# An MLP's first products for eight of sixteen groups placed in front, and the loads behind it put in another order

## The chip, the cores and the metric

The kernel runs on one core of a Trainium2 chip. The metric is the device time of one execution in microseconds. A core has TensorE (PE in the profile: matmuls and transposes, with PEld for its weight loads), VectorE (DVE), ScalarE (ACT), GpSimd (POOL) and SyncE (SP, which here only issues DMAs), each with its own queue of instructions that it works off in order, and 16 DMA engines.

## The reference

Two blocks run one after the other on 1024 tokens of width 1024: a hybrid layer with four attention-like branches, and a block that mixes, then applies an MLP and a gated projection. Only the end of the second block is touched:

```python
h = h + rms_norm_2(mix, g_mix_post[i])
hn = rms_norm_2(h, g_mlp_pre[i])
ff = jnp.square(jax.nn.relu(hn @ w_up[i])) @ w_down[i]      # 1024 -> 4096 -> 1024
h = h + rms_norm_2(ff, g_mlp_post[i])
gate = jax.nn.sigmoid(rms_norm_2(h, g_ple_pre[i]) @ w_ple_gate[i])
e = (p[i] @ w_ple_proj[i]) * gate
h = h + rms_norm_2(e, g_ple_post[i])
```

## The kernel before

**Products.** Every product is made in three matmuls: each operand is split into a high part (a rounded copy, `copy` at L147) and a low part (what is left, `sub_lo` at L157 on DVE or L155 on POOL), and high x high, high x low and low x high are summed in PSUM. Both big products of the MLP use a scheme with seven block products in place of eight; operands are formed as sums and differences of blocks on DVE.

**Order of the work.** The program is written in order, and a planner then lists the instructions of each engine: what stands earlier in the text has the higher priority, but an instruction whose inputs or buffer are not there by the planner's own clock is passed by. So loads written later can be issued earlier where a buffer is free. `issue_after` ties instructions of one engine behind a given one. All DMAs of the MLP are issued on SP's queue, except a few on ACT's.

**Buffers.** Tag "blk" has 31 slots of 4 KB a partition (`blk`, L93), shared by activations, operands, raw weights and norm tiles. Tag "w" has 9 slots (`NW`). PSUM banks come from four tags: "mm" 2, "s" 2, "t" 3, "o" 1. Pools opened for a stage take over the memory of the stage before once its tiles have been read.

**Before the MLP.** `out_phase` ends the mixing; `to_T` (L1201) transposes the first four token tiles into `hn`, eight slots of "blk". `t_pair` (L1655) reads two token tiles back, forms the operands t1 to t4 and b22 as differences (L1667 to L1670), transposes them (L274) and splits them: five operands of four slots each.

**Lead** (L1708 to L1720). For the first `LEAD` = 4 of 16 groups of 128 columns the two products that need only `hn` (`up_p1`, `up_p2`) are made ahead, while `t_pair` works; the results stay in `pa` (4 buffers).

**Up** (`up_group`, L1733). Each group loads its two weight halves (`wu`, 2 buffers, L1737), forms four sums (L1740 to L1743), makes the remaining products (five where the lead made two, else seven), evacuates them, applies relu and square, forms four combinations on POOL (L1786 to L1789), and stores seven arrays of 256 KB (L1792). The groups run from 0 to 15.

**Down** (L1881 to L1929). Two stages (groups 0 to 7, then 8 to 15) of seven products, with 96 matmuls each (L1919 to L1921). A stage loads sixteen 512 KB tiles of `w_down` (L1889), then for each product and quarter a left tile (L1908), and splits both. `evac_down` adds the products into `acc` (L1837). The products of a stage stand in the order

```python
order = (("a11", "b11"), ("s2", "t2"), ("s3", "t3"), ("a22", "t4"), ("s1", "t1"), ("s4", "b22"), ("a12", "b21"))
```

**Norm and gate.** After the fifth product of stage two the token tiles 4 to 7 are complete: `finish_mlp` (L1815) reads the residual, multiplies by the gain on POOL (L1824), scales and adds on DVE (L1827), and norms for the gate (L1225); its transposes follow the next product. Tiles 0 to 3 come after the last product. `ple_weights` (L1803) loads and splits a half of the gate's weights: half 0 ahead of the sixth product in "blk" slots (raw, high and low: twelve), half 1 at the end in "w" slots. Then sixteen gate products (24 matmuls each) run by tile, 4 to 7 and 0 to 3, with `evac_ple` (L1937) and `finish_ple` (L1950).

Of the kernel before, what the change touches and what calls it, by code (L numbers as in the profile page):

```python
# [27 lines left out]
_T = dict(STA='s', XN1=0, PWT=1, PO='0x1', PO2={}, PS=2, PSX=0, PSE='a', PB=99, PEA=(0, 1, 4), WB=8, XL=3, CLO='p', STE=None, STW=None, ST1='b', ST2='b', PLP='pvv', WLO2='p', QXP=1, LW='vp', LEAD=4, FD={0: 'g', 1: 'b', 6: 'g'}, FW=(0, 2), AG=0, PREO=(0, 2, 1), PMB=0, PWB=1, PM=3, SG=2, FA={(0, 2): 'g', (0, 3): 'mmm', (0, 7): 'qm', (1, 0): 'gg', (1, 6): 'gz'}, FB={(0, 3): 'm', (0, 7): 'qm', (1, 3): 'm', (1, 5): 'z', (1, 7): 'm'}, FC={(0, 3): 'mm', (0, 7): 'q', (1, 3): 'zm', (1, 6): 'm'}, NORM='v', NORM2='v', CS=8, MM=2, SB=2, TB=3, OB=1, WHI='aaav', WLO='pv', PTH='a', NW=9, NBLK=31, PTB=2, XN=1, AS=(2, 4, 6, 7), CPP=2, CALT=1, WORK='s0 A A A A A A A A s1 q t B c B B c c B p w B 5 6b c c c 4 0a 1a g 6a 7 3a 2 e e c c c B e B c B 1b e 0b 3b', KS=(2, 0, 3, 1))  # L28
# [48 lines left out]
def hybrid_then_mix_kernel(ctx: ExitStack, tc, I, c1, c2, out, dbg=None, upto=99):  # L77
# [1577 lines left out]
    def t_pair(t):  # L1655
# [15 lines left out]
        for name, src in (("t1", d[:, k1]), ("b22", xb[:, k2]), ("t2", e[:, k1]), ("t3", d[:, k2]), ("t4", e[:, k2])):  # L1671
# [6 lines left out]
            for kp in range(2):  # L1678
                s3 = tp[:, kp * 256:kp * 256 + 256].rearrange("p (k t) -> p k t", k=2)
                copy(hi[kp][:, :, o:o + P], s3, "a")  # L1680
                sub_lo(lo[kp][:, :, o:o + P], s3, hi[kp][:, :, o:o + P], "v")

# [25 lines left out]
    lead = []  # L1708
    for g in range(_T["LEAD"]):
# [23 lines left out]
    def up_group(g):  # L1733
# [10 lines left out]
        if g >= len(lead):  # L1744
# [4 lines left out]
            pa, a = up_tile(), mmb()  # L1749
            up_p1(pa, a, wa)  # L1750
        else:
            pa = lead[g]
        h23, s23 = wslot((2, 4, P)), wslot((2, 4, P))
        copy(h23[:], f23[:], "a")
        sub_lo(s23[:], f23[:], h23[:])
        b, c = stb(), trb()
        ub = blk(F32, (P, 2, 512))
        last = product(b[:], lambda k: (h23[:, 0, k], s23[:, 0, k]), right("t2"), True)
        ve.tensor_tensor(ub[:, 0], b[:], pa[:, 0], op=ALU.add)
        product_done(last)  # L1760
        if g >= len(lead):
            up_p2(pa, a, wa)
        last = product(b[:], lambda k: (h23[:, 1, k], s23[:, 1, k]), right("t3"), False)
        ve.tensor_tensor(ub[:, 1], b[:], pa[:, 0], op=ALU.add)
        product_done(last)
        h14, s14 = wslot((2, 4, P)), wslot((2, 4, P))
        copy(h14[:], f14[:], "a")
        sub_lo(s14[:], f14[:], h14[:])
        last = product(c[:], lambda k: (h14[:, 0, k], s14[:, 0, k]), right("t1"), True)
        ve.tensor_tensor(ub[:, 1], c[:], ub[:, 1], op=ALU.add)  # L1770
        product_done(last)
        h22 = wslot((2, 4, P))
        copy(h22[:, 0], a22, "a")
        sub_lo(h22[:, 1], a22, h22[:, 0])
        last = product(b[:], lambda k: (h22[:, 0, k], h22[:, 1, k]), right("t4"), False)
        ve.tensor_tensor(pa[:, 0], b[:], pa[:, 0], op=ALU.add)
        product_done(last)
        last = product(c[:], lambda k: (h14[:, 1, k], s14[:, 1, k]), right("b22"), False)
        ve.tensor_tensor(ub[:, 0], c[:], ub[:, 0], op=ALU.add)
        product_done(last)  # L1780
# [4 lines left out]
        us = [cur[0].tile([P, 512], F32, name=nm("us"), tag="us", bufs=6) for _ in range(3)]  # L1785
# [8 lines left out]
    for g in range(NG):  # L1794
        up_group(g)
# [87 lines left out]
    for stage in range(2):  # L1883
# [114 lines left out]
```

## Time and profile before

| | |
|---|---|
| median of three runs | 2416.91 us (2416.34 to 2417.73) |
| profiled execution | 2414.97 us |
| span of its profile | 2413.0 us |
| granted TensorE clock, mean | 0.970 |
| PE, DVE, ACT, POOL busy | 94%, 62%, 40%, 26% |
| HBM read, written | 191.04 MB, 68.70 MB |

The span runs from the first to the last instruction. The profile gives for each instruction its start, its duration and, in brackets, how long its engine had stood idle before it and what ended that. A PE matmul's duration overlaps that of the next, so that PE's time is better read from distances between starts. The MLP with the gate takes the last third of the span.

### The profile page before, as it was taken

How to read it: one execution, taken by the hardware profiler on the slowest of the kernel's cores; microseconds unless marked ns; L12 is line 12 of the kernel's file. 1: busy time of each engine (PE TensorE's matmuls, PEld its weight loads, DVE VectorE, ACT ScalarE, POOL GpSimd, SP SyncE). 2: the span in 40 equal slices, each digit the busy share in tenths (PEclk: the TensorE clock that was granted, in tenths of full speed). 3: DMA queues.
4: the chain of work that ended last, by engine and by line, in shares of the span. 5: the costliest groups of instructions: out<-in, count | busy, mean ns of one | idle time of the engine just before them, and what ended most of it. 6: DMA issues, size and time to landing. Idle time of an engine off the chain costs nothing. (4 is left out here: it accounts for less than half of the span.)

```text
span 2413.0 us, 30314 instructions
## 1 busy us (share of the span) xinstructions
PE 2256.5 (94%) x11004; PEld 1866.0 (77%) x11004; DVE 1497.1 (62%) x2837; ACT 960.3 (40%) x1926; POOL 633.1 (26%) x527
## 2 busy tenths in 40 slices
PE   7999999999998999999988988998999979998798
PEld 6788888888977788778867876776788858886577
DVE  7634466665578666344698666656655565866663
ACT  6212344444555444222312444443444433343442
POOL 4222100111357332343312233111333310002141
PEclk9999999999999999999999998998999989999889
DMA  9432111121134242242202110444444485441232
GB/s 331 135 96 75 43 62 62 62 70 59 35 122 140 68 144 80 82 143 90 81 27 79 49 35 33 159 150 141 160 152 149 144 302 175 124 146 57 68 120 88
DMA packets 192224, 261.72 MB, mean 108 GB/s; under 512 B 16510, under 2 KB 119494, under 8 KB 192074
## 3 DMA queue, kind: packets, MB, share of 16 engines
q1 hardware_dynamic: 183680, 246.94, 31.5%
q10 hardware_dynamic: 8394, 12.84, 1.7%
q8 instruction: 87, 1.43, 0.3%
q14 instruction: 63, 0.52, 0.1%
HBM read 191.04 MB, written 68.70 MB: 108 GB/s over the span
## 5 line engine op out<-in xcount | busy, mean ns | idle before, releaser
L229 PE MATMUL mm<-blk,wh 128*128 128x512 f32 x1264 | 506.1, 401 | 25.7 <-DVE blk L157 8.9
L230 PE MATMUL mm<-blk,wh 128*128 128x512 f32 x1264 | 502.8, 398 | 0.6 <-DVE blk L157 0.6
L231 PE MATMUL mm<-blk,wl 128*128 128x512 f32 x1264 | 501.6, 397 | 1.5 <-POOL wl L155 1.5
L229 PEld LDWEIGHTS mm<-blk,wh 128*128 128x128 f32 x1264 | 239.4, 189 | 79.2 <-issue 14.2
L155 POOL TENSOR_TENSOR wl<-wr,wh 128x1024 fp32r<-128x1024 f32 (+2 forms) x71 | 177.3, 2499 | 423.7 <-ACT wh L147 206.6
L231 PEld LDWEIGHTS mm<-blk,wl 128*128 128x128 f32 x1264 | 239.5, 190 | 51.0 <-POOL wl L155 2.0
L230 PEld LDWEIGHTS mm<-blk,wh 128*128 128x128 f32 x1264 | 239.8, 190 | 47.3 <-DVE blk L157 1.0
L229 PE MATMUL mm<-wh,blk 128*128 128x512 f32 (+3 forms) x616 | 224.3, 366 | 6.5 <-DVE fl L149 2.1
L230 PE MATMUL mm<-wl,blk 128*128 128x512 f32 (+3 forms) x616 | 222.4, 361 | 7.9 <-DVE wl L157 5.5
L231 PE MATMUL mm<-wh,blk 128*128 128x512 f32 (+3 forms) x616 | 220.7, 359 | 1.1 <-DVE blk L157 1.1
L157 DVE SCALAR_TENSOR_TENSOR wh<-blk,wh 128x1024 fp32r<-128x1024 f32 x112 | 133.1, 1222 | 81.5 <-issue 64.4
L147 ACT ACTIVATE wh<-blk 128x1024 fp32r<-128x1024 f32 x112 | 112.7, 1053 | 173.2 <-PE s L1920 92.0
L147 ACT ACTIVATE blk<-mm 64x512 fp32r<-64x512 f32 (+3 forms) x138 | 78.1, 569 | 160.9 <-PE mm L231 112.4
L157 DVE SCALAR_TENSOR_TENSOR PT<-t,PT 128x512 fp32r<-128x512 f32 (+3 forms) x224 | 111.4, 515 | 46.5 <-ACT PT L147 45.5
L147 ACT ACTIVATE PT<-t 128x512 fp32r<-128x512 f32 (+3 forms) x224 | 95.3, 460 | 110.0 <-PE o L814 70.2
L230 PEld LDWEIGHTS mm<-wl,blk 128*128 128x128 f32 x616 | 117.7, 191 | 27.4 <-DVE wl L157 7.3
L229 PEld LDWEIGHTS mm<-wh,blk 128*128 128x128 f32 x616 | 117.6, 191 | 27.1 <-issue 2.3
L147 ACT ACTIVATE wh<-wr 128x1024 fp32r<-128x1024 f32 (+2 forms) x92 | 94.6, 1030 | 101.1 <-DMA wr<-in_w_in_dram 21.6
L231 PEld LDWEIGHTS mm<-wh,blk 128*128 128x128 f32 x616 | 117.2, 190 | 19.2 <-DVE blk L157 1.9
L825 POOL TENSOR_TENSOR blk<-blk,ju 128x128 f32<-128x128 f32 x64 | 34.5, 539 | 279.4 <-DVE blk L824 279.3
L1332 DVE SCALAR_TENSOR_TENSOR blk<-blk,dwc,blk 128x512 f32<-128x512 f32 (+23 forms) x124 | 102.7, 881 | 0.4
L1148 POOL TENSOR_TENSOR acc<-tz,acc 128x512 f32<-128x512 f32 x48 | 69.5, 1451 | 116.5 <-DVE tz L1147 82.3
(350 smaller groups left out, 4764.9 us busy)
## 6 DMA issues: line engine op xcount, KB each, us to landing
acc<-acc SPq DMA_DIRECT2D x96, 256.0 KB, 2.5
wr<-in_w_merge_dram SPq DMA_DIRECT2D x32, 512.0 KB, 4.1
wu<-in_w_up_dram SPq DMA_DIRECT2D x32, 512.0 KB, 5.3
blk<-in_w_down_dram SPq DMA_DIRECT2D x32, 512.0 KB, 5.3
blk<-ss SPq DMA_DIRECT2D x32, 512.0 KB, 3.3
wr<-in_w_in_dram SPq DMA_DIRECT2D x27, 512.0 KB, 4.0
ss<-us SPq DMA_DIRECT2D x48, 256.0 KB, 2.5
blk<-sa SPq DMA_DIRECT2D x24, 512.0 KB, 4.5
```

The source lines that it names most:

```text
L147: return ac.activation(dst, src, AF.Copy, scale=1.0 if scale is None else scale)
L155: po.tensor_tensor(lo, x, hi.bitcast(F32), op=ALU.subtract)
L157: ve.scalar_tensor_tensor(out=lo, in0=x, scalar=scale, in1=hi.bitcast(F32), op0=ALU.mult, op1=ALU.subtract)
L229: pe.matmul(dst, sh, mh, start=(i == 0), stop=False)
L230: pe.matmul(dst, sh, ml, start=False, stop=False)
L231: last = pe.matmul(dst, sl, mh, start=False, stop=(i == n - 1))
L825: po.tensor_tensor(dst, dst, u[:], op=ALU.add)
L1148: po.tensor_tensor(acc[:], t[:], acc[:], op=ALU.add)
L1332: ve.scalar_tensor_tensor(out=acc[:, c:c1], in0=u[:, c - l:c1 - l], scalar=w, in1=acc[:, c:c1], op0=ALU.mult, op1=ALU.add)
```

## The change

- The lead makes two products for groups 8 to 15 (`LEAD` = 8, `LED`). Both results are stored to DRAM at once (`p1_d`, and a11, which is an output anyway); `up_group` reads them back into `pa`. `t_pair` becomes a generator with five steps a tile pair; one step stands between a group's two products and two behind them.
- The groups run 0, 8, 1, 9, 2, 10, 3, 11, 4, 12, 5, 6, 7, 13, 14, 15. A prepared group makes its products in the order p6, p5, p7, p3, p4; p5 is copied to a tile of its own by ACT, and one sum on DVE is added. The other groups swap the last two.
- The loads of stage one of the down product are written into the last three groups, behind the evacuation of p6: eight raws in groups 13 and 14, and in group 15 the left tiles of the first product, four raws, the left tiles of the second, four raws. The raws of stage two are loaded in stage one from its fourth product on, four at each.
- `finish_mlp` multiplies by scale and gain in one DVE operation and adds the residual in a second one; POOL's multiplication goes. The transposes of tiles 4 to 7 stand in the last product, one tile behind each quarter; those of tiles 0 to 3 among the gate products.
- The gate's weights are split on ACT and DVE alone. Half 1 comes first, ahead of the last product, in "blk" slots (raw, high, low); half 0 behind the last product, high and low in "w" slots. The gate products start with half 1 of tiles 4 and 5.

```diff
-    lead = []
-    for g in range(_T["LEAD"]):
+    units = (u for t in range(4) for u in t_pair(t))
+    LED = range(NG - _T["LEAD"], NG)
+    p1_d = {g: dram.tile([P, 512], F32, name=f"p1_{g}", tag=f"p1_{g}", bufs=1) for g in LED}
+    for g in LED:
...
         up_p1(pa, a, wa)
-        if g == 0:
-            for t in range(3):
-                t_pair(t)
+        sy.dma_start(p1_d[g][:], pa[:, 0])
+        next(units, None)
         up_p2(pa, a, wa)
-        if g == 1:
-            t_pair(3)
-        lead.append(pa)
+        sy.dma_start(mlp_o["a11"][g // 2][:, g % 2, :], pa[:, 1])
+        for _ in range(2):
+            next(units, None)
+    for _ in units:
+        pass
...
+        led = g in LED
+        pa = up_tile()
+        if led:
+            sy.dma_start(pa[:, 0], p1_d[g][:])
+            sy.dma_start(pa[:, 1], mlp_o["a11"][g // 2][:, g % 2, :])
...
+        def p6():
+            last = product(b[:], lambda k: (h23[:, 0, k], s23[:, 0, k]), right("t2"), True)
+            with tc.issue_after(ve.tensor_tensor(ub[:, 0], b[:], pa[:, 0], op=ALU.add).ins):
+                hook()
+            product_done(last)
...
+        p6()
+        if led:
+            q5 = p5()
+            p7()
+            ve.tensor_tensor(ub[:, 1], q5[:], ub[:, 1], op=ALU.add)
+            p3()
+            p4()
+        else:
             up_p2(pa, a, wa)
+            sy.dma_start(mlp_o["a11"][g // 2][:, g % 2, :], pa[:, 1])
+            p7()
+            p5()
+            p4()
+            p3()
...
-    for g in range(NG):
-        up_group(g)
+    led, rest = list(LED), list(range(LED[0]))
+    seq = []
+    while rest:
+        seq.append(rest.pop(0))
+        if len(led) > 3:
+            seq.append(led.pop(0))
+    seq += led
+    hooks = {led[0]: lambda: load_raws(0, 0, 0), led[1]: lambda: load_raws(0, 0, 1),
+             led[2]: lambda: (first_left("a11"), load_raws(0, 1, 1), first_left("s2"), load_raws(0, 1, 0))}
+    for g in seq:
+        up_group(g, hooks.get(g, lambda: None))
...
     def ple_weights(n):
-        return half_w(kview(I["w_ple_gate_2"][0]), n, n == 0)
...
+            w.h[b], w.l[b] = [blk(F32R, (P, 2, 512)) if n else wslot((2, 512)) for _ in range(2)]
+            copy(w.h[b][:], raw[:], "a")
+            sub_lo(w.l[b][:], raw[:], w.h[b][:])
...
-        w = blk()
-        po.tensor_tensor(w[:], acc[t][:], gains["post"][:], op=ALU.mult)
         r = small(1)
         rstd_of(r[:], ss[:], D, 1e-6)
-        ve.scalar_tensor_tensor(out=acc[t][:], in0=w[:], scalar=r[:, 0:1], in1=X[:], op0=ALU.mult, op1=ALU.add)
+        ve.scalar_tensor_tensor(out=acc[t][:], in0=acc[t][:], scalar=r[:, 0:1], in1=gains["post"][:], op0=ALU.mult, op1=ALU.mult)
+        ve.tensor_tensor(acc[t][:], acc[t][:], X[:], op=ALU.add)
...
         for i, (sn, tn) in enumerate(order):
-            if stage == 1 and i == 5:
-                w_ple[0] = ple_weights(0)
+            if stage == 0 and i >= 3:
+                load_raws(1, *((0, 0), (0, 1), (1, 1), (1, 0))[i - 3])
+            if stage == 1 and i == 6:
+                w_ple = [None, ple_weights(1)]
...
+                if xn4 and i == 6:
+                    to_T(hg, 4 + q, xn4[4 + q])
...
+    w_ple[0] = ple_weights(0)
     for t in range(4):
-        finish_mlp(t, 2 + t)
+        xn = finish_mlp(t)
+        later(4 + 2 * t, lambda t=t, xn=xn: to_T(hg, t, xn))
...
+    todo = [(4, 1), (5, 1), (4, 0), (5, 0), (6, 1), (6, 0), (7, 1), (7, 0)]
+    todo += [(t, j) for t in range(4) for j in range(len(pieces(t)))]
```

## Rows read from the trace of the kernel before

**Rows 1.** The page, busy time of PE: us, share, instructions.

```profile
PE 2256.5 (94%) x11004; PEld 1866.0 (77%) x11004; DVE 1497.1 (62%) x2837; ACT 960.3 (40%) x1926; POOL 633.1 (26%) x527
```

**Rows 2.** Windows: stretch, length, busy us (count) of engines, clock, DMA share, GB/s.

```profile
1593.70:1619.80 26.10, 26.04 (x130) 21.36 (x129) 15.96 (x30) 14.37 (x32) 7.27 (x4) 1.00 0.54 174
1619.80:1644.50 24.70, 9.72 (x50) 7.35 (x48) 16.65 (x38) 10.85 (x29) 0.00 (x0) 0.65 0.37 96
1644.50:1938.90 294.40, 292.62 (x1248) 236.05 (x1248) 174.53 (x200) 132.29 (x189) 94.69 (x60) 0.99 0.48 157
1938.90:1963.20 24.30, 6.96 (x20) 5.02 (x20) 22.23 (x16) 6.10 (x7) 7.82 (x4) 0.58 1.04 399
1963.20:2220.20 257.00, 257.00 (x1135) 212.60 (x1133) 168.40 (x172) 97.02 (x102) 0.93 (x1) 1.00 0.43 137
2220.20:2243.50 23.30, 0.16 (x2) 0.01 (x1) 17.48 (x17) 8.16 (x13) 17.21 (x10) 0.59 0.21 68
2243.50:2413.00 169.50, 151.83 (x664) 123.20 (x664) 93.43 (x143) 61.22 (x124) 41.97 (x34) 0.91 0.27 90
```

**Rows 3.** Timeline of PE, lead and first gap: start, us, engine, line, idle before.

```profile
1602.52 0.60 PE L274 MATMUL t<-c,row 128*128 128x128 f32 x4
...
1603.74 0.48 PE L1650 MATMUL mm<-blk,wh 128*128 128x512 f32 x1
...
1632.30 2.79 PE L274 MATMUL t<-c,row 128*128 128x128 f32 x12 [0.51 <-DVE blk L157]
1644.49 0.79 PE L1650 MATMUL s<-blk,wh 128*128 128x512 f32 x1 [9.39 <-ACT wh L147]
```

**Rows 4.** Timeline of SP's queue, first gap and groups behind it.

```profile
1635.13 25.38 SPq L1737 DMA_DIRECT2D wu<-in_w_up_dram  x8
...
1676.94 5.57 SPq L1792 DMA_DIRECT2D ss<-us  x3
```

**Rows 5.** Timeline of DVE, the first forming sum.

```profile
1641.39 0.69 DVE L1740 TENSOR_TENSOR wh<-wu 128x512 f32<-128x512 f32 x1 [4.54 <-DMA wu<-in_w_up_dram]
```

**Rows 6.** Timeline of SP's queue, second gap.

```profile
1932.09 7.33 SPq L1889 DMA_DIRECT2D blk<-in_w_down_dram  x8
1939.98 1.69 SPq L1908 DMA_DIRECT2D blk<-sa  x2
```

**Rows 7.** Timeline of ACT, second gap.

```profile
1951.19 4.84 ACT L147 ACTIVATE wh<-blk 128x1024 fp32r<-128x1024 f32 x5 [10.21 <-DMA blk<-sa]
```

**Rows 8.** Timeline of PE, third gap.

```profile
2243.50 1.65 PE L1919 MATMUL t<-wh,wh 128*128 128x512 f32 x3 [23.14 <-ACT wh L147]
```

**Rows 9.** Timeline of SP's queue ahead of the third gap.

```profile
2182.11 18.07 SPq L194 DMA_DIRECT2D wr<-in_w_ple_gate_dram  x4
2211.74 22.53 SPq L1908 DMA_DIRECT2D blk<-ss  x4
```

**Rows 10.** Timeline of POOL, third gap.

```profile
2219.27 6.99 POOL L1824 TENSOR_TENSOR blk<-acc,blk 128x1024 f32<-128x1024 f32 x3 [270.31 <-DVE acc L1837]
```

**Rows 11.** Timeline of DVE, third gap and behind it.

```profile
2218.36 2.48 DVE L1837 TENSOR_TENSOR acc<-mm,acc 128x512 f32<-128x512 f32 x4 [6.65 <-PE mm L1921]
...
2226.80 3.35 DVE L1827 SCALAR_TENSOR_TENSOR acc<-blk,sm,blk 128x1024 f32<-128x1024 f32 x1 [3.50 <-POOL sm L307]
...
2239.10 1.27 DVE L1827 SCALAR_TENSOR_TENSOR acc<-blk,sm,blk 128x1024 f32<-128x1024 f32 x1
...
2252.79 2.35 DVE L157 SCALAR_TENSOR_TENSOR wh<-blk,wh 128x1024 fp32r<-128x1024 f32 x2
...
2269.98 2.41 DVE L157 SCALAR_TENSOR_TENSOR blk<-t,blk 128x256 fp32r<-128x256 f32 x6 [0.45 <-ACT blk L147]
```

**Rows 12.** Timeline of PE, its last matmul.

```profile
2405.36 0.28 PE L231 MATMUL mm<-wh,blk 128*128 128x256 f32 x1
```

**Rows 13.** The page, DMA issues: count, KB each, us to landing.

```profile
acc<-acc SPq DMA_DIRECT2D x96, 256.0 KB, 2.5
```

More of the change, by code (lines that the diff above doesn't have):

```diff
@@ L1755, in up_group @@
         sub_lo(s23[:], f23[:], h23[:])
+        h14, s14 = wslot((2, 4, P)), wslot((2, 4, P))
         b, c = stb(), trb()
         ub = blk(F32, (P, 2, 512))
[L1758 to L1761, printed above, removed]
-            up_p2(pa, a, wa)
-        last = product(b[:], lambda k: (h23[:, 1, k], s23[:, 1, k]), right("t3"), False)
-        ve.tensor_tensor(ub[:, 1], b[:], pa[:, 0], op=ALU.add)
@@ L1765, in up_group @@
[L1765 to L1775, printed above, removed]
@@ new lines, in p7, with p5 @@
+        def p7():
+            last = product(b[:], lambda k: (h23[:, 1, k], s23[:, 1, k]), right("t3"), False)
+            ve.tensor_tensor(ub[:, 1], b[:], pa[:, 0], op=ALU.add)
+            product_done(last)
+        def p5():
+            copy(h14[:], f14[:], "a")
+            sub_lo(s14[:], f14[:], h14[:])
+            last = product(c[:], lambda k: (h14[:, 0, k], s14[:, 0, k]), right("t1"), True)
+            if led:
+                q5 = us_tile()
+                copy(q5[:], c[:], "a")
+            else:
+                ve.tensor_tensor(ub[:, 1], c[:], ub[:, 1], op=ALU.add)
+            product_done(last)
+            return q5 if led else None
@@ new lines, in p4, with p3 @@
+        def p4():
+            h22 = wslot((2, 4, P))
+            copy(h22[:, 0], a22, "a")
+            sub_lo(h22[:, 1], a22, h22[:, 0])
+            last = product(b[:], lambda k: (h22[:, 0, k], h22[:, 1, k]), right("t4"), False)
+            ve.tensor_tensor(pa[:, 0], b[:], pa[:, 0], op=ALU.add)
+            product_done(last)
+        def p3():
+            last = product(c[:], lambda k: (h14[:, 1, k], s14[:, 1, k]), right("b22"), False)
+            ve.tensor_tensor(ub[:, 0], c[:], ub[:, 0], op=ALU.add)
+            product_done(last)
@@ L1784, in up_group @@
             relu2(x_)
-        us = [cur[0].tile([P, 512], F32, name=nm("us"), tag="us", bufs=6) for _ in range(3)]
+        us = [us_tile() for _ in range(3)]
         po.tensor_tensor(us[0][:], ub[:, 0], ub[:, 1], op=ALU.add)
@@ L1803, in ple_weights @@
     def ple_weights(n):
-        return half_w(kview(I["w_ple_gate_2"][0]), n, n == 0)
+        src, w = kview(I["w_ple_gate_2"][0])[:, :, n * 512:(n + 1) * 512], W()
+        w.h, w.l = {}, {}
+        for b in range(4):
+            raw = blk(F32, (P, 2, 512))
+            sy.dma_start(raw[:], src[:, 2 * b:2 * b + 2, :])
+            w.h[b], w.l[b] = [blk(F32R, (P, 2, 512)) if n else wslot((2, 512)) for _ in range(2)]
+            copy(w.h[b][:], raw[:], "a")
+            sub_lo(w.l[b][:], raw[:], w.h[b][:])
+        w.hi = lambda k, c0, c1: w.h[k // 2][:, k % 2, c0:c1]
+        w.lo = lambda k, c0, c1: w.l[k // 2][:, k % 2, c0:c1]
+        return w
     def bcast2(ap):
@@ L1813, in hybrid_then_mix_kernel, with finish_mlp @@
     gains = {}
[L1815 removed]
+    def finish_mlp(t):
         if not gains:
@@ L1938, in evac_ple @@
         cs = slice(c0, c1)
-        if j == 0:
+        if t not in row:
             row[t] = blk()
@@ L1962, in finish_ple @@
             sy.dma_start(out[t * P:(t + 1) * P, cs], rw)
[L1964 to L1971 removed]
+    todo = [(4, 1), (5, 1), (4, 0), (5, 0), (6, 1), (6, 0), (7, 1), (7, 0)]
+    todo += [(t, j) for t in range(4) for j in range(len(pieces(t)))]
+    open_ = {t: len(pieces(t)) for t in range(NT)}
+    for t, j in todo:
+        c0, c1 = pieces(t)[j]
+        m = mmb()
+        last = gemm_N(m[:, :c1 - c0], hg, t, w_ple[c0 // 512], c0 % 512, c0 % 512 + c1 - c0)
+        evac_ple(t, j, c0, c1, m[:, :c1 - c0])
+        product_done(last)
+        open_[t] -= 1
+        if not open_[t]:
+            finish_ple(t)
     ph.close()
```

68 lines of the change are left out of this document (32 added, 36 removed).

## Prediction

> **What bounds the kernel now.** I read the page's busy shares first, then a table of stretches from the first product of the MLP to the end, then the timelines of single engines around each stretch where TensorE (PE) stands still. The shares say that PE is busy for 94% of the span [rows 1], so a change that removes no matmul can only win back what is left. The table shows where that is [rows 2]. From 1593.7 to 1619.8 us, from 1963.2 to 2220.2 us and nearly all the way between 1644.5 and 1938.9 us PE has no hole. Three stretches stand out: 1619.8 to 1644.5 (9.7 us busy of 24.7), 1938.9 to 1963.2 (7.0 of 24.3) and 2220.2 to 2243.5 (0.2 of 23.3). In each of them the granted clock falls to 0.58 to 0.65.
>
> A stretch without holes gives the price of a matmul of 512 columns: 257 us for 1135 of them is 0.2264 us [rows 2]. In the first stretch 26.1 us hold 8 products of 12 matmuls and ten sets of four transposes; a set costs 0.41 us (three sets in the 1.22 us from 1602.52 to 1603.74) [rows 3], so a matmul there takes (26.1 - 4.1) / 96 = 0.229 us.
>
> **First gap.** PE does the last transposes of the second half's operands until 1635.1, then waits 9.4 us [rows 3]. The loads of the next weights are issued only at 1635.13, when the pool whose memory they take has been read for the last time [rows 4], the first forming sum starts at 1641.39 behind that load [rows 5], and the first product at 1644.49. Products that need none of this would fill the time; the kernel has only those of four groups.
>
> **Second gap.** Sixteen loads of the second matrix stand ahead of the first loads of the left operands on SP's queue: the last eight are issued from 1932.09, the left ones not before 1939.98 [rows 6]. The copy that PE needs starts at 1951.19, after 10.2 us of waiting for that DMA [rows 7], while the 16 DMA engines run at their limit (share 1.04, 399 GB/s) [rows 2].
>
> **Third gap.** PE waits 23.1 us for a copy of the sixth product's left operand [rows 8]. The gate's weights were loaded at 2182, the left operands not before 2211.7, over 22.5 us [rows 9]: gate raws, their splits and the norm's tiles took the shared slots of the tag "blk" first. The norm's work on GpSimd (2.3 us a row block) then stands in the way [rows 10], and beside it a VectorE operation takes 3.35 us that takes 1.27 us alone [rows 11].
>
> **Part by part.** No matmul and no transpose is added or removed. So each part is priced as a hole that closes.
>
> (a) *Eight groups in front, new order.* The lead grows from 8 to 16 products: 16 x 12 x 0.229 = 44.0 us, with 20 sets of transposes 8.2 us, so it ends at 1593.7 + 52.2 = 1645.9. The transposes are spread three steps to a group and end in the seventh group, some 5.5 to 8 us before the lead does. The 9.4 us from last transpose to first product [rows 3] then lie mostly beside products; I leave 3 us (bounds 0 and 9.4). Eight groups of 5 products and eight of 7 follow: 96 x 12 x 0.229 = 263.8 us. Before, 104 products should take 285.8 of the 294.4 us from 1644.5 on [rows 2], so 8.6 us were lost to preparation; with one of the prepared groups behind each of five ordinary ones, and products of one bank no longer next to each other, I keep 4. End: 1645.9 + 3 + 263.8 + 4 = 1916.7 instead of 1938.9: **22 us won** (bounds 14 and 29).
>
> What it adds is hidden or small. Sixteen stores of 256 KB and sixteen loads of the same size use DMA engines at a share of 0.48 to 0.54 [rows 2], and such a load lands in 2.5 us [rows 13], with four buffers to start it early. ScalarE gets a copy of 512 columns in eight groups, VectorE one sum (0.69 us [rows 5]); they are busy 174.5 and 236 of 294.4 us [rows 2]. If that cover goes, a group waits for about what it added, 0.7 us, 6 us in all; this is inside the bounds.
>
> (b) *Loads of the second product earlier.* During the last three groups no product reads the first operand's eight slots, so eight raw loads fit there; in the last group each finished product frees four slots, first for the left operands. Needed from the first of these groups to the end of the first down product: 16 raws and 8 left loads of 0.524 MB and three groups' own 3.15 MB (weights 1.05, reload 0.52, stores 1.57) are 22.0 MB. At the 399 GB/s of [rows 2] that is 55 us; the time is 3 x 60 x 0.229 + 96 x 0.2264 = 62.9 us. So it fits, with the first operands at the head. The gap holds 24.3 - 20 x 0.2264 = 19.8 us of loss [rows 2]; I leave 4 for the change of banks and the differences formed on VectorE: **16 us won** (bounds 8 and 20).
>
> The Trainium skill speaks against this part: "DMA: Bandwidth & Descriptors", section Specifications, gives some 358 GB/s from HBM for a core. By that the 22.0 MB would need an estimated 61.5 us, all of the time there is. The trace disagrees, with 399 GB/s over 24.3 us, and the measurement decides.
>
> (c) *Norm and gate.* The rest of the kernel from the end of the fifth product of the second half (2220.2) lasts 192.8 us. PE's own work there: two products 2 x 96 x 0.2264 = 43.5; the gate's 384 matmuls 87.9; 16 sets of transposes 6.6; from PE's last matmul to the end of the span 2413 - 2405.7 = 7.3 [rows 12]. Sum 145.3, so at most 47.5 us can be won. I count slots: right operands 8, left ones up to 8, residual rows 4, gains 2 make 22 of 31, and one half of the gate's weights needs 8, with its raws in passing; the other half now goes to the other tag. So the sixth product's loads get their slots in time and PE need not stand still.
>
> Then VectorE is the next to be late, because the multiplication moves from GpSimd to it. Prices [rows 11]: an evacuation 0.64 (four in 2.48), a split 1.18, a transposed piece's split 0.40, a norm row block three operations of at most 1.28 and small ones, 4.1. During the sixth product: 3 of evacuations left over, 4 x 4.1 norm, 8 x 1.18 splits = 28.8 against PE's 21.7. During the seventh: 2.6 + 32 x 0.40 + 8 x 1.18 + 4 x 1.18 (gate) = 29.5 against 25.0 with transposes. During the first eight gate products: 2.6 + 4.7 + 16.4 + 12.8 and 4 x 3.5 for the gate's own half-size operations = 50.5 against 47.3. The excess is 7.1 + 4.5 + 3.2 = 15 us. **32 us won** (bounds 0 and 47.5).
>
> **Sum.** 22 + 16 + 32 = 70 us. The profiled execution took 2414.97 us, its span 2413.0 us; 2414.97 - 70 = 2345. The median of the runs, 2416.91, lies 1.9 us above that execution, so I forecast 2347 us.
>
> **Rivals.** (1) *All holes close*: VectorE's excess is caught up later, when it has less to do, and (a) and (b) come near their upper bounds: 29 + 20 + 44 = 93 us, 2324 us. For it: during the gate of the last four tiles VectorE has time. Against it: 15 us of excess in just these stages.
>
> (2) *The norm goes first.* The order on VectorE is the planner's, and the norm of four row blocks is traced ahead of the sixth product's splits. If all of it goes first, PE waits about 16.4 us there, and as long again for the second four: 33 us instead of 15, and ScalarE's part of the chain adds some. (c) then gives some 10 us: 2369 us. For it: the norm's operation at 2226.80 runs well ahead of these splits [rows 8, 11]; against it: at 2252.79 splits stand amid the norm's operations [rows 11].
>
> (3) *The early loads don't move.* They sit at the same queue, and the planner gives slots by its own times; if no slot comes free before the last group ends, (b) gives nothing and the change does not do what it says there: 2363 us.
>
> (4) *Slower.* SP works in order. If the reload of a prepared group and the next weights are queued behind stores that wait for GpSimd, as three stores do over 5.57 us [rows 4], each of eight groups waits 5.57 + 2.5 [rows 13] + 4 x 0.69 [rows 5] = 10.8 us, 87 us in all: 2347 + 87 = 2434 us. It decides from 70 / 8 = 8.8 us a group on. Against it: four buffers allow the reload a group earlier, and no group of before waits so long.
>
> **How the numbers follow.** Forecast 0.58, rival (1) 0.13, (2) 0.18, (3) 0.07, (4) 0.04. A measurement of this kernel tells about 0.2% (4.8 us) from no change. Faster holds everything but (4) with a little of (2): 0.95; (4) is split between slower, 0.03, and, with what closes less than the bounds say, the same, 0.02. The range runs from 2325, where (1) begins, to 2385, where (2) ends with (a) and (b) at their lower bounds.
>
> **What would show it.** PE without a hole over 4 us between 1620 and 1660, and the first down product at about 1921 instead of 1953. Left operands issued before the last raws. No wait over 5 us ahead of the sixth product of the second half, and VectorE busy over 90% from there to the eighth gate product. The forecast is wrong if PE waits for a reload in the groups, if the raw loads are still issued after the last stores, or if a copy or a split of the sixth product again ends a wait of over 15 us.

## The result, and the profile after

The changed kernel takes **2356.56 us** (median of 4 runs, 2355.97 to 2359.79) against 2416.62 us (2416.15 to 2417.73) for the kernel before beside it: ratio 0.9754, 95% interval 0.9737 to 0.977. The forecast was 2347.0 us, so 60 us were won where 70 were expected. The profiled execution is the slowest of the four: 2359.79 us, span 2358.0 us.

The page of after, busy time by engine; it answers to [rows 1]:

```profile
PE 2250.1 (95%) x11004; PEld 1866.0 (79%) x11004; DVE 1501.6 (64%) x2846; ACT 962.7 (41%) x1935; POOL 608.8 (26%) x517
```

No matmul came or went. VectorE has nine instructions more and GpSimd ten fewer, eight of them the norm's multiplications that moved. The windows of after, cut where the holes begin and end, answer to [rows 2] (columns: stretch, length, busy us and count of PE, PEld, DVE, ACT and POOL, clock, DMA share, GB/s):

```profile
1598.50:1653.20 54.70, 53.67 (x273) 43.91 (x271) 34.90 (x62) 30.40 (x69) 9.48 (x6) 1.00 0.53 172
1653.20:1664.00 10.80, 2.36 (x5) 1.45 (x6) 5.84 (x10) 4.12 (x7) 0.00 (x0) 0.59 0.81 218
1664.00:1935.40 271.40, 271.40 (x1177) 222.28 (x1175) 178.91 (x200) 128.74 (x186) 97.24 (x60) 0.99 0.61 202
1935.40:1960.00 24.60, 18.75 (x67) 14.65 (x67) 23.25 (x18) 8.26 (x10) 12.02 (x4) 0.86 0.68 251
1960.00:2200.60 240.60, 240.29 (x1061) 198.64 (x1060) 167.99 (x172) 96.66 (x101) 0.00 (x0) 1.00 0.46 147
2200.60:2227.60 27.00, 27.00 (x121) 22.36 (x120) 24.09 (x30) 11.29 (x15) 2.71 (x5) 1.00 0.37 117
2227.60:2240.00 12.40, 6.67 (x31) 4.89 (x29) 10.51 (x21) 9.58 (x21) 1.45 (x3) 0.68 0.48 146
2240.00:2358.00 118.00, 109.98 (x516) 90.72 (x514) 67.68 (x113) 43.11 (x95) 21.46 (x25) 0.98 0.24 83
```

Busy time alone misleads in a hole, since a matmul takes longer at the low clock (0.63 us in place of 0.39 at 1663.46 us, in a stretch with a granted clock of 0.59). So I count **loss**: the length of a stretch, less 0.2275 us for each matmul of 512 columns that starts in it (between the 0.2264 and 0.229 us of the prediction), half of that for one of 256 columns, and 0.1025 us for each transpose (0.41 / 4). From 1653.2 to 1664.0 five matmuls leave 10.8 - 1.1 = 9.7 us. By this measure the part around the first gap lost 20.5 us before (1593.9 to 1644.5) and 12.7 after (1598.5 to 1664.0), the groups behind it 10.7 and 4.1, the second gap 20.0 and 9.6, and everything from the end of the fifth product of the second half on (tail included) 55.2 and 20.0. Expectations below give 21.9 and 12.0, 8.8 and 3.8, 20.1 and 9.7 for the first three pairs; the counts here are the ones that follow from the rule. The last part took 192.8 us before and takes 157.4.

Three holes are left: the first between the lead and the groups, the second in the first down product, the third in the seventh product of the second half. PE's timeline of after (start, duration, engine, line, operation, idle time before and who ended it):

```profile
1652.12 1.03 PE L274 MATMUL t<-c,row 128*128 128x128 f32 x8
1658.65 0.79 PE L1650 MATMUL mm<-blk,wh 128*128 128x512 f32 x1 [5.49 <-ACT wh L147]
...
1662.86 0.80 PE L1650 MATMUL s<-blk,wh 128*128 128x512 f32 x1 [3.00 <-ACT wh L147]
...
1937.91 0.49 PE L1990 MATMUL mm<-wh,wh 128*128 128x512 f32 x1 [2.30 <-DVE wh L157]
...
1954.23 0.50 PE L1990 MATMUL mm<-wh,wh 128*128 128x512 f32 x1 [3.56 <-DVE wh L157]
...
2237.72 1.22 PE L1989 MATMUL mm<-wh,wh 128*128 128x512 f32 x2 [1.85 <-ACT wh L147]
```

The waits of 9.39, 10.21 (ScalarE's, for a DMA) and 23.14 us [rows 3, 7, 8] became 5.49 + 3.00, 2.30 + 3.56 and a set of short ones. One number needs a caution: the first product of the lead starts at 1598.49 us, before at 1593.94, though nothing ahead of it was edited. In the traces of all changed kernels this start lies between 1592.98 and 1602.84 us. So the table below also gives the time from that first product to the end of the span of the profiled execution, which is free of it. It is one execution of each kernel, and not free of all scatter: the changed kernel, profiled twice (after and again), took 759.5 and 763.6 us. What is smaller than these 4 us is read from the stretch that an edit touches.

| kernel | median us | ratio to before, 95% interval | first product to end, us |
|---|---|---|---|
| before | 2416.62 | 1 | 819.1 |
| after | 2356.56 | 0.9754 [0.9737, 0.977] | 759.5 |
| lead4 | 2373.44 | 0.9809 [0.978, 0.9837] | 772.7 |
| nohooks | 2367.53 | 0.979 [0.9758, 0.9822] | 769.0 |
| oldnorm | 2394.55 | 0.9895 [0.9859, 0.9931] | 794.9 |
| wublk | 2349.79 | 0.9706 [0.9672, 0.9741] | 751.4 |
| again (after, beside tie, wuvec, tieT) | 2360.55 | 0.9778 [0.9765, 0.9792] | 763.6 |
| tie | 2354.52 | 0.9753 [0.9739, 0.9766] | 753.9 |
| wuvec | 2338.86 | 0.9688 [0.9674, 0.9701] | 740.9 |
| tieT | 2365.22 | 0.9791 [0.9777, 0.9805] | 761.7 |
| pull | 2333.90 | 0.9658 [0.9644, 0.9672] | 737.0 |
| noX | 2340.95 | 0.9684 [0.9666, 0.9703] | 738.9 |
| pulltie | 2336.14 | 0.9662 [0.9646, 0.9677] | 734.4 |
| pullmul | 2344.38 | 0.9705 [0.9692, 0.9718] | 745.6 |

### The profile page after: what moved, and what is told of

Read it like the earlier page. It is cut to its first block, busy times and chain, and to the rows that moved or that the text cites. A ratio compares the mean times of both kernels' runs of the same rounds, so it can differ in the third digit from the quotient of the medians.

```text
span 2358.0 us, 30343 instructions
## 1 busy us (share of the span) xinstructions
PE 2250.1 (95%) x11004; PEld 1866.0 (79%) x11004; DVE 1501.6 (64%) x2846; ACT 962.7 (41%) x1935; POOL 608.8 (26%) x517
## 4 chain that ended last, share of the span: by engine, by line
PE 45%; DVE 7%; DMA 2%; ACT 1%; issue 1%; POOL 0%; DVEq 0%; POOLq 0%; ACTq 0%; SPq 0%
PE mm L229 6%; PE mm L230 6%; PE mm L231 6%; DVE blk L1332 3%; PE s L1650 2%; PE s L1652 2%; PE s L1651 2%; PE t L274 2%; PE t L1650 1%; PE t L1652 1%; PE t L1651 1%; PE mm L1990 1%; PE mm L1650 1%; PE mm L1652 1%; PE mm L1991 1%; PE t L1990 1%
## 5 line engine op out<-in xcount | busy, mean ns | idle before, releaser
L155 POOL TENSOR_TENSOR wl<-wr,wh 128x1024 fp32r<-128x1024 f32 (+2 forms) x69 | 169.8, 2462 | 399.3 <-ACT wh L147 184.7
L229 PE MATMUL mm<-wh,blk 128*128 128x512 f32 (+3 forms) x544 | 197.8, 365 | 7.1 <-DVE fl L149 3.5
L231 PE MATMUL mm<-wh,blk 128*128 128x512 f32 (+3 forms) x544 | 194.9, 360 | 1.1 <-DVE blk L157 1.1
L157 DVE SCALAR_TENSOR_TENSOR wh<-blk,wh 128x1024 fp32r<-128x1024 f32 x116 | 140.2, 1237 | 62.4 <-issue 49.2
L230 PE MATMUL mm<-wl,blk 128*128 128x512 f32 (+3 forms) x480 | 170.5, 356 | 5.5 <-DVE wl L157 4.8
L307 POOL TENSOR_TENSOR sm<-sm,mhalf 128x1 f32<-128x1 f32 x64 | 37.5, 590 | 423.9 <-DVE sm L306 408.4
L147 ACT ACTIVATE wh<-wr 128x1024 fp32r<-128x1024 f32 (+2 forms) x89 | 91.5, 1030 | 93.4 <-DMA wr<-in_w_in_dram 21.9
L229 PEld LDWEIGHTS mm<-wh,blk 128*128 128x128 f32 x544 | 103.9, 191 | 24.2 <-issue 3.6
L231 PEld LDWEIGHTS mm<-wh,blk 128*128 128x128 f32 x544 | 104.1, 191 | 17.1 <-DVE blk L157 1.9
L230 PEld LDWEIGHTS mm<-wl,blk 128*128 128x128 f32 x480 | 92.3, 192 | 19.3 <-DVE wl L157 6.4
```

The lines of the kernel that those rows point to most:

```text
L147: return ac.activation(dst, src, AF.Copy, scale=1.0 if scale is None else scale)
L155: po.tensor_tensor(lo, x, hi.bitcast(F32), op=ALU.subtract)
L157: ve.scalar_tensor_tensor(out=lo, in0=x, scalar=scale, in1=hi.bitcast(F32), op0=ALU.mult, op1=ALU.subtract)
L229: pe.matmul(dst, sh, mh, start=(i == 0), stop=False)
L230: pe.matmul(dst, sh, ml, start=False, stop=False)
L231: last = pe.matmul(dst, sl, mh, start=False, stop=(i == n - 1))
```

## The experiments

**One part undone at a time: lead4, nohooks, oldnorm.** lead4 goes back to four groups in front:

```diff
-LEAD=8
+LEAD=4
-        next(units, None)
+        for _ in range(15 if g == LED[0] else 0):
+            next(units, None)
-        for _ in range(2):
+        for _ in range(5 if g == LED[1] else 0):
             next(units, None)
```

> The changed kernel with four groups in front instead of eight, and the token blocks' preparation where it stood before (three of them inside the first group, the fourth inside the second). The spills, the order that puts one prepared group early and three last, and everything behind stay. Theory: the eight groups in front gained 15 us (loss in the first gap 21.9 to 12.0 us, stalls of the up groups 8.8 to 3.8 us), and the other parts don't depend on it: 2368 to 2372 us, with the first hole of the kernel before (some 20 us of loss) back between the lead and the first up group, and nothing changed from 1925 us on but the offset. Rival: the 5 us of the up groups come from the order of the groups and not from their number, so only 10 us come back: 2365 to 2367 us. Second rival: the length of the lead counts for nothing and the preparation would have been hidden by the steps alone: within 3 us of 2356.6.

Measured 2373.44 us, 1.4 us above the first theory's range, and 13.2 us more from the first product to the end. PE waited for the preparation again, in many pieces (of 40 us from 1620 it was busy 26.33), and the up groups lost some 0.2 us in every 10. From the first product of the lead to the first down product the loss is 27.6 us, with the change 16.5: the longer lead gives 11 us. The rest lies in the second hole (12.5 us of loss in place of 9.6), which the theory held to be unchanged. GpSimd, ScalarE and PE there (L1826 is the first of the last group's four sums):

```profile
1952.01 15.64 POOL L1826 TENSOR_TENSOR us<-blk 128x512 f32<-128x512 f32 x1 [12.00 <-ACT blk L1698]
1976.02 1.09 ACT L147 ACTIVATE acc<-mm 128x512 f32<-128x512 f32 x2 [13.89 <-issue]
1978.59 1.65 PE L1990 MATMUL t<-wh,wh 128*128 128x512 f32 x3 [6.31 <-ACT wh L147]
```

What holds GpSimd up there is the subject of wublk and wuvec below.

nohooks takes the loads out of the groups:

```diff
-        up_group(g, hooks.get(g, lambda: None))
+        up_group(g, lambda: None)
+            if stage == 0 and i == 0:
+                for k in ((0, 0), (0, 1), (1, 1), (1, 0)):
+                    load_raws(0, *k)
```

> The changed kernel without the early loads: the first stage's second factors are loaded where the second product begins, in one go, and the left tiles when they are asked for, as before the change. Theory: the early loads gained 10 us (loss behind the up groups 20.1 to 9.7 us): 2365 to 2369 us, with the hole at the start of the second product back at 17 to 20 us. Rival: a tile scheduler issues the loads as soon as buffers are free wherever they stand in the program, so their place is worth little, and the 10 us come from the new group order: within 3 us of 2356.6, and the loads of the first factors leave in the same 10 us as with the change.

Measured 2367.53 us, inside the theory's range, and 9.5 us more from the first product on. SP's queue and then PE in that trace:

```profile
1908.52 0.94 SPq L1839 DMA_DIRECT2D blk<-in_w_down_dram  x2
...
1912.12 13.73 SPq L1839 DMA_DIRECT2D blk<-in_w_down_dram  x14
1926.84 1.69 SPq L1845 DMA_DIRECT2D blk<-sa  x2
```

```profile
1939.61 1.22 PE L1992 MATMUL mm<-wh,wh 128*128 128x512 f32 x2 [14.63 <-ACT wh L147]
```

Fourteen raw loads stand ahead of the left ones, as in [rows 6]. SP's queue with the change has the first raws in the groups, and left tiles ahead of the last raws:

```profile
1885.27 2.06 SPq L1839 DMA_DIRECT2D blk<-in_w_down_dram  x4
...
1913.73 0.88 SPq L1845 DMA_DIRECT2D blk<-sa  x2
...
1918.33 1.99 SPq L1839 DMA_DIRECT2D blk<-in_w_down_dram  x4
```

The rival that the tile scheduler moves the loads anyway falls.

oldnorm puts back the old `finish_mlp`, `ple_weights` and tile order:

```diff
+        w = blk()
+        po.tensor_tensor(w[:], acc[t][:], gains["post"][:], op=ALU.mult)
-        ve.scalar_tensor_tensor(out=acc[t][:], in0=acc[t][:], scalar=r[:, 0:1], in1=gains["post"][:], op0=ALU.mult, op1=ALU.mult)
-        ve.tensor_tensor(acc[t][:], acc[t][:], X[:], op=ALU.add)
+        ve.scalar_tensor_tensor(out=acc[t][:], in0=w[:], scalar=r[:, 0:1], in1=X[:], op0=ALU.mult, op1=ALU.add)
...
+            if stage == 1 and i == 5:
+                w_ple[0] = ple_weights(0)
```

> The changed kernel with the norm and the gate as before: GpSimd's multiplication back in the norm, the gate's weights loaded in halves by the old helper (the first before the sixth product, the second behind the last), transposes behind one later product, the tiles of the gate in the old order. Theory: that part gained 34 us (from the end of the fifth product to the end of the kernel 192.6 to 157.4 us): 2388 to 2393 us, with loss of some 23 us in the sixth product and 13 us behind the seventh. Rival: a part of the 34 us came from the earlier parts (buffers that are free earlier): 2375 to 2385 us.

Measured 2394.55 us (2385.60 to 2400.19), 1.5 us above the theory's range, and 35.4 us more from the first product on. PE's wait of [rows 8] is back to the hundredth:

```profile
2223.53 1.65 PE L1981 MATMUL t<-wh,wh 128*128 128x512 f32 x3 [23.14 <-ACT wh L147]
```

The three parts together give 13.2 + 9.5 + 35.4 = 58.1 of the 59.6 us between before and after. They add up within the scatter of 4 us, though not quite apart: some 3 us of lead4's 13.2 lie in the second hole, which its edit does not touch.

**The first hole: wublk.** The weights of the first up group are loaded during the sixth group in front, into two of the general buffers:

```diff
+        if g == LED[5]:
+            for fh in range(2):
+                r = blk(F32, (P, 8, P))
+                sy.dma_start(r[:], w_up[:, :, fh * 2048:fh * 2048 + P])
+                pre.append(r)
```

> The changed kernel with the weights of the first up group in two tiles of the general buffers, loaded during the sixth group in front, not in the pool that opens only when the preparation's pool has closed. Theory: the 9.7 us of loss between the lead and the up groups are the pool's hand-over: the loads of the first group's weights are issued only at 1653.2 us, behind the last transposes' pool, land 4.4 us later, and a copy, the forming and a split stand behind them; loaded in front, the group's first product follows the lead at once and its sixth product waits for little: 7 to 9 us faster than the changed kernel, 2348 to 2350 us. Rival: the last transposes (12 to 15 us of a pair of token blocks with two buffers) end with the lead whatever the weights do, and the sixth product needs them: 0 to 3 us faster, 2354 to 2357 us, with the wait moved to the transposed tiles.

Measured 2349.79 us, and PE has no wait from 1650 to 1670. The pool opens no earlier than with the change. SP's first loads into it, of after and then of wublk:

```profile
1653.18 1.01 SPq L1744 DMA_DIRECT2D wu<-in_w_up_dram  x2
```

```profile
1656.51 4.12 SPq L1753 DMA_DIRECT2D wu<-in_w_up_dram  x4
```

The transposes still run to the end, too, but the first group now covers both. So the hand-over is the loads behind the pool, as the theory said, and the rival falls.

The same trace shows something new. The second hole grew to 12.6 us of loss, from 9.6. GpSimd, then VectorE, then ScalarE, then PE (L1835 is the first of the last group's four sums; L1923 is the differences):

```profile
1930.86 17.90 POOL L1835 TENSOR_TENSOR us<-blk 128x512 f32<-128x512 f32 x1 [11.57 <-ACT blk L1698]
1948.84 1.29 POOL L1836 TENSOR_TENSOR us<-us,pa 128x512 f32<-128x512 f32 x1
```

```profile
1942.98 3.49 DVE L1923 TENSOR_TENSOR blk<-blk,blk 128x1024 f32<-128x1024 f32 x3
1946.39 1.22 DVE L157 SCALAR_TENSOR_TENSOR wh<-blk,wh 128x1024 fp32r<-128x1024 f32 x1
1957.89 1.22 DVE L157 SCALAR_TENSOR_TENSOR wh<-blk,wh 128x1024 fp32r<-128x1024 f32 x1 [10.28 <-ACT wh L147]
```

```profile
1955.34 1.08 ACT L147 ACTIVATE acc<-mm 128x512 f32<-128x512 f32 x2 [14.33 <-issue]
```

```profile
1957.91 1.65 PE L1999 MATMUL t<-wh,wh 128*128 128x512 f32 x3 [7.84 <-ACT wh L147]
```

A sum that takes 1.29 us ends only when VectorE's unbroken run ends (1947.6). The store of the group's last sum is issued at 1952.60, and 2.7 us later ScalarE copies the first bank into an accumulator. By the code the accumulators' pool takes the memory of the sums' pool, so I read the 14.33 us, for which the profile names no releaser, as the wait for that store; the second product's copies stand behind it.

**GpSimd or VectorE: wuvec.** On top of wublk the four sums of the last group move to VectorE:

```diff
-        po.tensor_tensor(us[0][:], ub[:, 0], ub[:, 1], op=ALU.add)
+        (ve if g == seq[-1] else po).tensor_tensor(us[0][:], ub[:, 0], ub[:, 1], op=ALU.add)
...
```

> The kernel with the first up group's weights in general buffers, and the four sums of the last up group on VectorE in place of GpSimd. In the trace without that edit a sum of 128x512 that elsewhere takes 1.3 us on GpSimd took 17.90 us, 1930.86 to 1948.84, over just the stretch in which VectorE worked without a pause (1921 to 1947.6); its stores, the pool's closing and the copies of the first product's banks followed, and TensorE waited 7.84 us for ScalarE. Theory: GpSimd gets no access beside a VectorE that never pauses, and that is the 12.7 us hole: with 2.8 us of sums on VectorE the hole falls to 2 to 5 us, 7 to 10 us faster than the 2349.8 us without the edit: 2340 to 2343 us. Rival: the hole is VectorE's own load, to which 2.8 us are added: 2349 to 2353 us.

Measured 2338.86 us. VectorE is busy all of the 20 us from 1930 to 1950 (17.61 of 19 from 1930 on in wublk), and yet PE has one wait of 2.29 us left in the second hole, 2.5 us of loss in place of 12.6. The rival falls: here VectorE's load cost nothing, GpSimd's exclusion did.

**The order of the differences: tie.** The changed kernel, with each quarter's differences behind a split of the first product:

```diff
+                    with tc.issue_after(split[min(q + 2, 3)].ins):
                         add(t1[:], b12[:], b11[:], ALU.subtract)
                         ...
```

> The changed kernel with one order on VectorE: the differences for the second product of a quarter queued behind the split of the first product's quarter two further on (at most the last). Theory: the second hole (9.6 us of loss) is VectorE's order, nine differences of 1.17 us standing ahead of the first product's splits while the engine has room over both products: 4 to 7 us faster than the changed kernel. Rival: something else that is late stands behind the differences, the sums of the last group on GpSimd, whose tiles' pool must close before the accumulators' pool opens and the first product can be evacuated: 0 to 2 us faster, with the wait between the first and the second product.

Measured 2354.52 us against 2360.55 for the unaltered kernel beside it, 6 us, as the theory said; loss in the second hole 4.3 us. VectorE in the changed kernel, whose last row ends the wait of 3.56 us at 1954.23, and two of GpSimd's sums beside it:

```profile
1933.23 3.49 DVE L1913 TENSOR_TENSOR blk<-blk,blk 128x1024 f32<-128x1024 f32 x3
...
1940.64 3.50 DVE L1913 TENSOR_TENSOR blk<-blk,blk 128x1024 f32<-128x1024 f32 x3
1944.20 2.17 DVE L157 SCALAR_TENSOR_TENSOR wh<-blk,wh 128x1024 fp32r<-128x1024 f32 x1
1946.30 6.75 DVE L1913 TENSOR_TENSOR blk<-blk,blk 128x1024 f32<-128x1024 f32 x3
1952.97 1.21 DVE L157 SCALAR_TENSOR_TENSOR wh<-blk,wh 128x1024 fp32r<-128x1024 f32 x1
```

```profile
1939.86 5.43 POOL L1825 TENSOR_TENSOR us<-blk 128x512 f32<-128x512 f32 x1 [12.00 <-ACT blk L1698]
...
1947.48 2.27 POOL L1828 TENSOR_TENSOR blk<-pa,blk 128x512 f32<-128x512 f32 x1
```

Three differences take 6.75 us beside GpSimd's sums and 3.49 us from 1933.23 on, where GpSimd stands idle, so order and GpSimd both have a part in the hole. The new order has a price: the second product of the second half, which waits for nothing in the changed kernel, now waits 1.64 us for a split (at 2112.03).

The unaltered changed kernel beside them:

> The changed kernel unaltered, as the base on the same chip for the three runs beside it: 2354 to 2360 us, with the three holes of its first trace (12, 9.7 and 9 us of loss) at the same places.

It took 2360.55 us, half a microsecond above that range, with the same holes (12.1, 10.6 and 9.8 us of loss, by the same cuts 12.7, 9.6 and 9.9 in the first trace).

**The third hole: tieT, pull, noX.** For this hole I take the loss over the whole seventh product. The seven traces that leave it as it is (after, lead4, nohooks, wublk, again, tie, wuvec) have 9.4 to 9.9 us there, so that 1 us can be told apart. tieT queues the transposes of a block behind their quarter, on PE alone:

```diff
-                    to_T(hg, 4 + q, xn4[4 + q])
+                    with tc.issue_after(last.ins):
+                        to_T(hg, 4 + q, xn4[4 + q])
```

> The changed kernel with the transposes of each of blocks 4 to 7 queued on TensorE behind the quarter of the seventh product after which the program has them. In the changed kernel the transposes of three blocks stand between the first and the second quarter, and the loss of 9 us lies there (2227.6 to 2240). Theory: the hole is the order on TensorE and, behind it, on ScalarE and VectorE, whose copies for the second quarter stand behind those of the transposes: 5 to 7 us faster than the changed kernel. Rival, as forecast: VectorE has more work than time there (17.5 of 20 us busy from 2200 to 2240), so the hole only moves to a later quarter: 0 to 2 us faster.

Measured 2365.22 us (2359.47 to 2366.21) against 2360.55 (2359.14 to 2364.11) beside it: not faster, a miss for the theory and for the rival. The seventh product lost 12.4 us. PE had only one block's transposes in the way and waited all the same. PE, then ScalarE in that trace:

```profile
2239.42 1.22 PE L1989 MATMUL mm<-wh,wh 128*128 128x512 f32 x2 [9.17 <-ACT wh L147]
```

```profile
2237.28 1.06 ACT L310 ACTIVATE blk<-acc 128x1024 f32<-128x1024 f32 x1 [2.11 <-DVE acc L1904]
2238.24 0.19 ACT L310 ACTIVATION_READ_ACCUMULATOR blk<-acc 128x1 f32 x1
2238.33 3.88 ACT L147 ACTIVATE wh<-blk 128x1024 fp32r<-128x1024 f32 x4
```

The copies for the second quarter are queued on ScalarE behind a norm's sum of squares, which waits for VectorE. So pull, on top of wuvec, acts there: the transposes of the block before go behind the next quarter's splits.

```diff
+                if xn4 and i == 6 and q:
+                    with tc.issue_after(high.ins), tc.issue_after(low.ins):
+                        to_T(hg, 3 + q, xn4[3 + q])
```

> The kernel with the first group's weights loaded in front and the last group's sums on VectorE (2338.9 us, loss of 9.3 us between the first and the third quarter of the seventh product), and the transposes of blocks 4 to 7 moved one quarter back, behind the splits of the next quarter on ScalarE and VectorE. With the transposes tied on TensorE alone the hole stayed (TensorE waited 9.17 us for ScalarE's copies of the second quarter, which stand behind the transposes' copies and the norms' sums on ScalarE). Theory: that order is the hole; now the second quarter's copies come first: loss of 1 to 4 us in place of 9.3, 2331 to 2334 us. Rival, as forecast: VectorE has more work than time in these 40 us, so the loss moves to later quarters or to the gate: 2337 to 2340 us.

Measured 2333.90 us, loss 3.2 us in place of wuvec's 9.6 (9.3 in the expectation), and the wait that is left is VectorE's:

```profile
2217.81 0.51 PE L2003 MATMUL mm<-wh,wh 128*128 128x512 f32 x1 [2.72 <-DVE wh L157]
```

noX, also on top of wuvec, leaves out `ve.tensor_tensor(acc[t][:], acc[t][:], X[:], op=ALU.add)` for `t >= 4`:

> The kernel with the first group's weights loaded in front and the last group's sums on VectorE (2338.9 us), without the addition of the residual for blocks 4 to 7, which is left out: four instructions of 1.22 us less on VectorE in the stretch of the third hole, and nothing else. If VectorE's work is what fills that stretch, the hole loses what the engine loses, 4 to 5 us: 2334 to 2335 us. If the hole is the order of ScalarE's copies, which stand behind a chain of sums, roots and scalings, only the links that are in the chain of the last block in front of the copies count, 1 to 2.5 us: 2336.5 to 2338 us.

The median, 2340.95 us, is above both ranges and no help: in the profiled execution the first product started at 1602.84 us, 5.9 us later than in wuvec. In the seventh product the loss is 7.7 us, 1.9 less than in wuvec, while VectorE lost 4.9 us of work. In the stretch itself that is the second expectation, the order on ScalarE.

**All mends, and the multiplication: pulltie, pullmul.** pulltie adds the order of the differences (`split[min(q + 1, 3)]`) to pull:

> All mends together: the first group's weights loaded in front, the last group's sums on VectorE, the transposes of blocks 4 to 7 one quarter back, and the differences for the second product queued behind the split of the quarter after. Without the last of these the first down product loses 3 to 4 us waiting for VectorE's split of its first and second quarter (2.29 us in one wait), with four differences of 1.17 us standing ahead of it. Theory: that order is the rest of the second hole: 2 to 3 us faster than 2333.9: 2331 to 2332 us, the best of all kernels. Rival: the second product then finds its differences late and waits in its turn: 2333 to 2336 us.

Measured 2336.14 us against pull's 2333.90, with intervals that cover each other: no gain is shown, and the theory's 2331 to 2332 us is missed. The second hole is down to 0.9 us of loss from 4.2, but as in tie the second product of the second half now waits for a split, which costs about 2 us there:

```profile
2104.34 0.50 PE L2006 MATMUL t<-wh,wh 128*128 128x512 f32 x1 [1.37 <-DVE wh L157]
```

From the first product on it is the shortest of all, 734.4 us against 737.0, which is within the scatter. pullmul gives GpSimd its multiplication back, on top of pull:

```diff
+        po.tensor_tensor(acc[t][:], acc[t][:], gains["post"][:], op=ALU.mult)
-        ve.scalar_tensor_tensor(out=acc[t][:], in0=acc[t][:], scalar=r[:, 0:1], in1=gains["post"][:], op0=ALU.mult, op1=ALU.mult)
-        ve.tensor_tensor(acc[t][:], acc[t][:], X[:], op=ALU.add)
+        ve.scalar_tensor_tensor(out=acc[t][:], in0=acc[t][:], scalar=r[:, 0:1], in1=X[:], op0=ALU.mult, op1=ALU.add)
```

> The same without the differences' order (2333.9 us), with one step of the change undone: the norm's multiplication by the gain back on GpSimd, eight instructions of 128x1024, so that VectorE has one pass less for each block and GpSimd one more in the chain of each norm. Theory: beside a VectorE that is busy 17 to 18 of 20 us, GpSimd's pass takes 3 us and more and holds up VectorE's own, so the chain of a norm is longer by 3 us or more a block and the third hole opens again: 2336 to 2342 us. Rival: VectorE's work is what fills the stretch, and it loses 1.28 us a block: 2329 to 2333 us.

Measured 2344.38 us: 10.5 us slower than pull, though VectorE has a pass less for each block, and above both ranges. GpSimd, then VectorE, at the same time, then PE and ScalarE at the place that opened, far more in the gate (9 us of loss from 2260 to 2280) than in the third hole (5.3 us in place of 3.2):

```profile
2200.40 2.41 POOL L1913 TENSOR_TENSOR acc<-acc,blk 128x1024 f32<-128x1024 f32 x1 [1.25 <-ACT scr L310]
```

```profile
2200.45 3.43 DVE L1225 SCALAR_TENSOR_TENSOR blk<-acc,sm,blk 128x1024 f32<-128x1024 f32 x1
```

```profile
2274.02 0.80 PE L229 MATMUL mm<-blk,blk 128*128 128x512 f32 x1 [6.67 <-ACT blk L2033]
```

```profile
2273.37 1.09 ACT L2033 ACTIVATE blk<-mm 128x512 f32<-128x512 f32 x2 [7.68 <-DMA out_dram<-blk]
```

An operation of 1.28 us takes 3.43 us on VectorE beside GpSimd's 2.41, as the 3.35 us of [rows 11] did before. But that can account for the third hole at most, some 2 us. In the gate ScalarE waits 7.68 us for the store of finished rows, by the code the slot of "blk" that its next row takes; pull has no such wait. Why the slots fall that way with GpSimd's multiplication is not shown. So moving the multiplication to VectorE is a gain in this kernel, not a cost, but most of its size is not shown to come from the two engines hindering each other.

## Why the prediction was right, and where it was off

**Part (a), 22 us: about 14.** The preparation's stalls in the groups came out as put, 4.1 us of loss for the 4 kept. The lead itself took 54.7 us (1598.5 to 1653.2) in place of 52.2: the stretch that priced it, 1593.7 to 1619.8, holds eight sets of transposes and not ten, so a matmul there cost (26.1 - 3.3) / 96 = 0.2375 us and not 0.229, 1.6 us over 192. What failed is the term "the 9.4 us from last transpose to first product then lie mostly beside products; I leave 3 us". It measured 9.7. The transposes did not end in the seventh group, 5.5 to 8 us ahead: the last eight run at 1652.12, behind the last lead product, and the load that waits for their pool leaves at 1653.18. I had counted steps per group and not what a step waits for; what made the last steps late is not shown. wublk, which covers the loads behind the pool, takes out the whole 9.7 us.

**Part (b), 16 us: about 10.** The transfers fit, as the sum said: the first down product starts at 1923.49 us without a wait, amid the last up group's products, and one stretch of after shows how close it was:

```profile
1920.00:1940.00 20.00, 17.70 (x74) 14.13 (x74) 14.74 (x15) 11.75 (x17) 6.57 (x5) 0.96 1.03 398
```

It is the rate on which the sum rested. What failed is "I leave 4 for the change of banks and the differences formed on VectorE": 9.6 us. The differences stand ahead of the splits that PE waits for, and GpSimd's sums beside them stretch three from 3.49 to 6.75 us. tie shows the first, wuvec what GpSimd's sums cost.

**Part (c), 32 us: 35.** The size was right. The sixth product runs without a wait, as the counting of slots said, and oldnorm brings the 23.14 us back. The reason for what is left was mostly wrong, and that the size fits is in good part luck. I put 15 us down to VectorE's excess of work, 28.8 + 29.5 + 50.5 = 108.8 us in three stages; in these stages of after it is busy 19.5, 26.8 and 35.6 us, 82 in all, of 104.4 us. That is 79%, where the prediction named over 90% as a sign. The part took 157.4 us in place of PE's own 145.3, 12.1 us over, and pull, with the same instructions on every engine, saves 6.4 of the 9.6 us in the third hole. So at most about a third of that hole is work that VectorE cannot fit (it is busy 24.09 of 27.0 us during the sixth product and the quarter after it, 89%). The rest was the order of ScalarE's queue, a step that I had not seen at all.

**The sum.** 59.6 us in place of 70 leave 10.4, about the 8 and 6 us that (a) and (b) fell short, less the 3 that (c) gave beyond its 32. The profiled execution is 14.8 us over the 2345 of the sum; the other 4.5 are its later first product, ahead of every edit.

**The rivals.** Rival (4) fell: PE is busy 271.40 of 271.40 us in the groups, so no group waits for its reload. (3) fell with nohooks. (2) fell for the sixth product, but its thought, a norm's operation queued ahead of splits, turned out true on ScalarE and for the seventh product, at 6 us rather than 33. (1) did not come about, but is near: with the mends of pulltie the time from the first product on is 84.7 us shorter than before, where that rival gave 93. Those edits are not part of the change.

## What to carry to other kernels

Work placed in front to cover a hand-over covers it only if the loads behind the hand-over can be issued during that work: look at what memory they take, and who reads it last. When a wait names an engine that has room, ask which instruction stands ahead of the late one in that engine's queue, and move that before you take work away. And do not put work on GpSimd beside a VectorE that runs without pauses, if anything hangs on either of them.

## What the runs showed of the hardware

GpSimd can be kept out for much longer than one VectorE instruction: 17.90 us in wublk for a sum of 1.29 us, beside some fifteen of them in a row, and 15.64 us in lead4. The Trainium skill, "SBUF — State Buffer", section "Who interferes with whom", says that the one that comes second is blocked until the other's instruction ends. The 3.43 us of VectorE beside one GpSimd pass of 2.41 us agree with that; the 17.90 us go beyond it.

What ended these waits can be read from six traces. In a run without a pause each VectorE instruction starts some 0.08 us before the one ahead of it ends. The sum (5.43 us in after, 5.42 in again, oldnorm and tieT, 15.64 in lead4, 17.90 in wublk) ended 1.15 or 1.16 us behind the first place where that chain broke: a pause of 0.07 us in after (1944.14 to 1944.20 in the rows above), of 0.07 to 0.21 us in the next four, the end of the run in wublk. Once GpSimd was in, both were slow: in after its sums took 2.15 to 2.27 us and VectorE's operations of 1.2 us took 2.17 to 2.32 us. tie does not fit: its sum ended after 1.82 us, 1.16 us behind a VectorE instruction that the next one followed without a pause. Why GpSimd got in there is open.

The part ahead of the first product, which no kernel here edits, differs by up to 9.9 us between the profiled executions (1592.98 to 1602.84 us), and from the first product on two of the same kernel differ by 4.1 us. An edit worth 2 or 3 us shows only in the stretch that it touches.
